# A separate buffer for the outgoing mLSTM states, and new durations for the gate chain in the mixer's list scheduler

## The chip, the cores and the metric

The kernel runs on one core of one Trainium2 chip. The time is that of one execution on the device in microseconds (us). The profile speaks of five engines: PE is TensorE (PEld its weight loads), DVE is VectorE, ACT is ScalarE, POOL is GpSimd and SP is SyncE, which here issues the DMAs. Each engine works through its own instructions in the order in which they were written, so an instruction that waits holds up all behind it on its engine.

## What is computed

One step of a two-layer hybrid diffusion backbone: a feed-forward half, a mixer, a second feed-forward half, for 512 latent tokens and 128 context tokens (640 columns in all), with 1024 features. The mixer projects its input once (`z = u @ w_in`) and splits the columns among grouped-query attention (A), a bidirectional matrix memory (B, mLSTM, 4 heads of 64) and differential attention (C). The part that the change touches is B. In the reference:

```
gates = (gb + b_gates).reshape(B, L, 4, H_B)
ig = gates[:, :, 0::2]
logf = log_sigmoid(gates[:, :, 1::2])
b = cumsum(logf);  m_out = max(b + m, max(dlog))      # per chunk, both directions
num = (q k^T * exp(dlog - m_out)) v + w_inter * (q C)
h = num / max(|den|, exp(-m_out))
C_new = decay * C + sum_s wk * k v                    # the final states
h_b = h_f + rev(h_r)
return h_b, (stack([Cf, Cr]), stack([nf, nr]), stack([mf, mr]))
```

For the context tokens the final states `C`, `n` and `m` of both directions are outputs (`new_b_C`, `new_b_n`, `new_b_m`).

## The kernel before

Activations are held feature by token. Every fp32 product is made of three passes of a high and a low half (`mm3`), which makes TensorE the engine with the most to do. Each layer runs feed-forward, mixer, feed-forward; the mixer appears twice in the trace, once per layer.

Inside the mixer the order of the work of PE, ACT, DVE and POOL is set by a list scheduler (`Sched`), at build time. Each piece of work is an `op(engines, ns, fn, deps, dl, alloc, use)`: engines that can do it, an assumed duration in ns, what it depends on, a due time, and the buffers that it allocates or uses. `Sched.run` repeatedly takes the op that could start earliest by these assumed durations (ties by due time) and writes out its instructions. So a duration in an `op` changes no instruction; it changes where instructions stand in each engine's queue, and on which of two allowed engines a copy is put.

Two places matter here.

*The gate chain* (`gates`). The gate columns are projected on PE (`gps`), biased on ACT into `ig` and `lf`, and then go back and forth in seven steps over rows of 640 tokens: `c1`, `c2` on ACT (log-sigmoid into `tm`), `c3` on DVE (four scans, `ae`), `c4` on DVE (four scans, the running maximum), `c5` on ACT (`nM`), `c6` on DVE (`tm` and the small `mo`, `Ml`), `c7` on ACT (a table load, `ae`, `ws`). Then PE transposes `ae` and `ws` into PSUM (`aet`, lines 1557 to 1566). Meanwhile PE multiplies the other columns of `w_in`: one token tile and column chunk (`zps`) is 24 matmuls of 512 columns, evacuated by a copy into `z`, which then goes through the rotary multiplications (`m`, `yc`, `kc`) and splits (`qsC`, `ks`) on POOL, DVE and ACT. The tiles `zps` have four PSUM buffers with the transposes (`ps1`).

*The final states and the second direction.* For the context tokens `kw` (DVE) scales the keys, four small matmuls per direction make the states in PSUM, ACT copies them into the SBUF tile `cst`, and two DMAs write it out, `new_b_C` in rows of 64 numbers and `new_b_n` in single numbers of 4 bytes (`stc`, lines 2133 and 2134). The tile `cst` and the tile `hx` share one buffer (tag `hx`, one copy of it). `hx` is the quotient of the second direction of each head, made on DVE (line 2101) and added to the first direction's `hb` by POOL (line 2104); then `hsq` on ACT, `hss` on DVE, `hrr` on POOL normalise the head. The assumed duration of `stc` is 2000 ns, on the pseudo-engine Q that stands for DMAs.

```
            xb = buf("hx")
            ...
            o = op("D", dve(320), hx, (o,), dl - 3, (xb,), (b,))
            self.out = op("G", gps(320), ..., (o, self.out), dl, use=(xb,))
        ...
        cb, cbx = buf("hx"), {}
        ...
        bops = [op("Q", 2000, stc, co, dl, use=(cb,))]
```

The functions `act(n)`, `dve(n)` and `gps(n)` give assumed durations for n columns: 60 + 0.84 n, 66 + 1.05 n and 150 + 2.1 n ns.

Of the kernel before, what the change touches and what calls it, by code (L numbers as in the profile page):

```python
# [10 lines left out]
F32 = mybir.dt.float32  # L11
# [6 lines left out]
D = 1024  # L18
# [4 lines left out]
T = LAT + CTX  # L23
# [38 lines left out]
class Sched:  # L62
# [32 lines left out]
    def buf(self, pool):  # L95
        return Buf(pool)

    def op(self, eng, ns, fn, deps=(), dl=0.0, alloc=(), use=()):

        o = Op()  # L100
        o.ns = {eng: ns} if len(eng) == 1 else dict(zip(eng, ns))
        o.fn, o.dl, o.alloc, o.id, o.end, o.succ = fn, dl, alloc, self.n, None, []
        self.n += 1
        self.left += 1
        o.deps = [d for d in deps if d is not None]
        o.wait = 0
        for d in o.deps:
            if d.end is None:
                d.succ.append(o)
                o.wait += 1  # L110
        for b in (*alloc, *use):
            b.users.append(o)
        if not o.wait:
            self.ready.append(o)
        return o
# [66 lines left out]
class Net:  # L182
# [958 lines left out]
    def mixer(self, l, np_stack):  # L1141
# [71 lines left out]
        for nm, g in (("tq", gq), ("tk", gk)):  # L1213
            tb = zp.tile([P, 4, 2, 64], F32, name=nm, bufs=1)
            nc.vector.tensor_tensor(tb[:, :, 0, :], self.ropeA[:, :, 0, :], g.unsqueeze(1).to_broadcast([P, 4, 64]), ALU.mult)
            for e in range(2):
                o = 1 - e
# [21 lines left out]
        S = Sched({k: RS[k] for k in "ps1 ps2 pr pT ks z sqz m2 qsC QTc KTC hsqC".split()})  # L1239
        op, buf = S.op, S.buf  # L1240
        act = lambda n: 60 + 0.84 * n
        dve = lambda n: 66 + 1.05 * n
# [239 lines left out]
        def gates(rawb, wb, prev, dl):  # L1482
# [11 lines left out]
            o = op("G", 2500, g0, prev, dl, (rawb,))  # L1494
            o, o2 = split_ops(lambda: bx["raw"], [P, KD, P], wb, rawb, bx, (o,), dl)
            outs = []
            for hf in range(2):
                c0, c1 = HALF[hf]
# [13 lines left out]
                o = op("P", 24 * 0.42 * (c1 - c0), pe, (o, o2), dl, (pb,), (wb,))  # L1512
# [29 lines left out]
                nc.scalar.activation(ae[64 : 64 + R], tm, AF.Exp)  # L1542
                nc.scalar.activation(ws, ae[0:R, LAT:T], AF.Exp, bias=Ml)

            o = op("A", 2 * act(T), c1, outs, dl)
            o = op("A", act(T) + 1300, c2, (o,), dl)
            o = op("D", 4 * dve(T) + 250, c3, (o,), dl)
            o = op("D", 2 * dve(T) + 250, c4, (o,), dl)
            o = op("A", act(T), c5, (o,), dl)
            o = op("D", dve(T) + 400, c6, (o,), dl)  # L1550
            o = op("A", act(T) + act(CTX) + 1500, c7, (o,), dl)
            pb = buf("ps1")

# [23 lines left out]
        def split_ops(get, shape, wb, rawb, bx, deps, dl):  # L1577
            def hi():
                if wb.slot < 4:
                    H, L = self.wpair(shape, wb.slot)  # L1580
                else:
                    H, L = (zp.tile(shape, F32R, tag="w5" + x, name="w" + x, bufs=1) for x in "HL")
                nc.scalar.copy(H, get())
                bx["hl"] = (H, L)

            def lo():
                H, L = bx["hl"]
                nc.vector.tensor_tensor(L, get(), H.bitcast(F32), ALU.subtract)

            o1 = op("A", act(1024), hi, deps, dl, (wb,), (rawb,))  # L1590
            o2 = op("D", dve(1024), lo, (o1,), dl, use=(wb, rawb))
            return o1, o2
# [21 lines left out]
        for ci, (parts, post) in enumerate(chunks):  # L1614
            if ci == 1:
                def cache():
                    nc.sync.dma_start(ka[0], a["cache_a_k"][0, l])
                    nc.sync.dma_start(va[0], a["cache_a_v"][0, l])
                    nc.sync.dma_start(kc[0], a["cache_c_k"][0, l].rearrange("s h n d -> s (h n) d"))
                    nc.sync.dma_start(vc[0], a["cache_c_v"][0, l])  # L1620

                o = op("Q", 3000, cache, (), 0.0)
                for k in ("ka", "va", "kc", "vc"):
                    done[k, 0] = o
                rb, wb = buf("raw"), buf("w")
                pops += gates(rb, wb, (), clock)
# [23 lines left out]
            for t in range(NT):  # L1650
# [6 lines left out]
                o = lastpe  # L1657
                for kk in range(4):
                    def pe(kk=kk, t=t, bx=bx, pb=pb, hls=hls):
                        if kk == 0:  # L1660
                            bx["ps"] = self.ps1("zps", pb.slot)
                        project_k(bx["ps"], t, hls[kk]["hl"], kk)

                    o = op("P", 6 * 214, pe, (o, *(hops[kk] or ())), clock, (pb,) if kk == 0 else (), (wbs[kk],) if kk == 0 else (wbs[kk], pb))
# [8 lines left out]
        tc_ = []  # L1673
# [182 lines left out]
        tp = tp_stack.enter_context(self.pool("mlstm", 2, side="right"))  # L1856
# [65 lines left out]
        for i, (dst, q) in enumerate(((hb, 0), (kb, 1), (vb[:, :, :, 0:64], 2), (ob, 3))):  # L1922
            for t0_, t1_ in ((0, 2), (2, 5)) if q != 2 else [(t, t + 1) for t in range(NT)]:
# [4 lines left out]
                o = op("Q", RL + 3000 * i + t0 * 1e3, ld, (), t0 - 50)  # L1928
# [177 lines left out]
        self_sel, self_mask, self_ps1, self_mm = self.sel, self.mask, self.ps1, self.mm  # L2106
        heads = [Head(h) for h in range(4)]

        cb, cbx = buf("hx"), {}
        co = []  # L2110
        for d in range(2):
            b, kwb = buf("ps1"), buf("hsqB")

            def kwf(d=d):
                if d == 0:
                    cbx["cst"] = tp.tile([64, 8, 65], F32, tag="hx", name="cst", bufs=1)
                cbx["kw", d] = kw = tp.tile([P, NT, 64], F32, tag="hsq", name="kw", bufs=1)
                for h in range(4):
                    nc.vector.tensor_scalar(kw[:, h, :], kb[:, 4, h, :], wsT[:, 32 * d + h : 32 * d + h + 1], None, ALU.mult)

            def pe(d=d, b=b):
                cbx["ps", d] = ps = self.ps1("cst", b.slot)
                for h in range(4):
                    self.mm(ps[0:64, h * 65 : h * 65 + 65], cbx["kw", d][:, h, :], vb[:, 4, h, :], True, True)

            dl = t0 + 45 + 3 * d
            o = op("D", 600, kwf, (lds[1, 4], *done["aeT"], *co), dl, (cb, kwb) if d == 0 else (kwb,), () if d == 0 else (cb,))
            o = op("P", 900, pe, (o, lds[2, 4]), dl, (b,), (kwb,))
            co.append(op("A", 300, lambda d=d: nc.scalar.copy(cbx["cst"][:, 4 * d : 4 * d + 4, :], cbx["ps", d][0:64, 0:260].rearrange("p (h c) -> p h c", c=65)), (o,), dl, use=(b, cb)))
# [69 lines left out]
        for dd in range(2):  # L2199
# [7 lines left out]
            for e in range(2):  # L2207
# [20 lines left out]
                o = None  # L2228
                for i, c in enumerate(CORD):
                    for hf in range(2):  # L2230
# [8 lines left out]
                        o = op("P", 3 * 0.418 * w, pe, (o, o2, *yts[c, hf], *scs), t0 + L2 + 30 + 10 * d + i, (pb,) if o is None else (), (wb,) if o is None else (wb, pb))  # L2239
# [165 lines left out]
```

## Time and profile before

| | us |
|---|---|
| median of three runs | 2797.31 (2794.95 to 2800.3) |
| the profiled execution | 2793.09 |
| its span, first to last instruction | 2791.3 |
| PE busy | 2700.6 (97% of the span) |
| DVE busy | 2128.1 (76%) |
| ACT busy | 1285.6 (46%) |
| POOL busy | 308.6 (11%) |

The profiled execution is one run of the same program; its trace has start and duration of each instruction, and for idle time in front of an instruction the event that ended it. Besides busy time a stretch has a granted clock of TensorE, 1.00 for 2.4 GHz and 0.50 for 1.2 GHz. A busy share is an average over the whole span. Idle time of an engine is read from the waits and from the stretch in which it lies.

### The profile page before, as it was taken

Reading aid. Unit: us, or ns where it says so; the run is one execution under the profiler, and the core shown is the slowest. Engines: PE = TensorE matmul, PEld = TensorE weight load, DVE = VectorE, ACT = ScalarE, POOL = GpSimd, SP = SyncE. Lnnn points to the kernel's source line nnn. Section 1 sums busy time; section 2 is a strip of 40 time slices with the busy share of each in tenths; the row PEclk is TensorE's granted clock in tenths of the full one; section 3 lists DMA queues with packets and bytes.
Section 4 is the critical chain, followed back from the end, with each engine's and each line's share of the span. In section 5 each row is a group of like instructions: output and inputs, shape, how many; then the busy total and the mean of one; then the engine's idle time right before and its main releaser. Section 6 shows DMA issues by size and latency. Waiting matters only on the chain.

```text
span 2791.3 us, 46818 instructions
## 1 busy us (share of the span) xinstructions
PE 2700.6 (97%) x17869; PEld 2533.9 (91%) x17869; DVE 2128.1 (76%) x4618; ACT 1285.6 (46%) x2941; POOL 308.6 (11%) x504
## 2 busy tenths in 40 slices
PE   7999999999989999999989999999999999999998
PEld 5998999888889999999989999997888898999998
DVE  6687899776865578898987889988667647676765
ACT  5424334456666342433444334345657644343433
POOL 1000000142522100000010000003343220000000
PEclk8999999999999999999999999999999999999999
DMA  8444443322102334344333443442211033222232
GB/s 239 138 145 141 119 129 107 110 93 88 40 3 80 96 95 137 91 121 122 105 91 92 121 144 109 141 131 83 82 50 39 3 114 91 77 75 76 84 84 76
DMA packets 363352, 276.44 MB, mean 99 GB/s; under 512 B 25128, under 2 KB 350840, under 8 KB 363128
## 3 DMA queue, kind: packets, MB, share of 16 engines
q1 hardware_dynamic: 363128, 273.45, 32.8%
q8 instruction: 141, 2.31, 0.4%
q14 instruction: 83, 0.68, 0.1%
HBM read 259.25 MB, written 14.16 MB: 98 GB/s over the span
## 4 chain that ended last, share of the span: by engine, by line
PE 86%; DVE 6%; ACT 3%; DMA 2%; POOL 2%; issue 1%; SPq 0%; POOLq 0%; DVEq 0%; ACTq 0%
PE gu L192 35%; PE w L192 20%; PE zps L192 6%; PE ga L192 5%; PE wo L192 4%; PE tr L1293 3%; PE y L192 3%; PE sc L192 2%; PE num L192 2%; PE z L192 1%; PE adp L333 1%; DMA out_new_b_n<-cst 1%; PE adt L348 1%; DMA adaw<-in_w_ada 1%; PE st L192 1%
## 5 line engine op out<-in xcount | busy, mean ns | idle before, releaser
L192 PE MATMUL gu<-u,wH 128*128 128x320 f32 x3504 | 624.8, 316 | 8.3 <-DVE pm L669 3.7
L192 PE MATMUL w<-hid,wH 128*128 128x384 f32 (+1 forms) x2816 | 624.4, 312 | 1.9 <-ACT wH L212 1.1
L192 PEld LDWEIGHTS gu<-u,wH 128*128 128x128 f32 x3504 | 541.9, 190 | 33.9 <-ACT X L1005 7.9
L192 PE MATMUL gu<-u,wL 128*128 128x320 f32 x3120 | 565.6, 314 | 2.4 <-DVE wL L213 1.1
L192 PEld LDWEIGHTS gu<-u,wL 128*128 128x128 f32 x3120 | 482.8, 189 | 20.6 <-ACT X L1005 6.7
L192 PEld LDWEIGHTS w<-hid,wH 128*128 128x128 f32 x2816 | 471.8, 188 | 7.3 <-ACT hid L693 3.4
L192 PE MATMUL w<-hid,wL 128*128 128x256 f32 (+1 forms) x1408 | 432.1, 311 | 0.9 <-DVE wL L213 0.8
L192 PEld LDWEIGHTS w<-hid,wL 128*128 128x128 f32 x1408 | 264.7, 189 | 2.5 <-DVE wL L213 2.3
L221 ACT CAST wH<-raw 128x512 fp32r<-128x512 f32 x266 | 163.6, 620 | 205.5 <-PE w L192 91.8
L345 DVE SCALAR_TENSOR_TENSOR adacc<-adaw,cs,adacc 128x256 f32<-128x256 f32 x602 | 255.0, 477 | 0.0
L192 PE MATMUL zps<-wH,u 128*128 128x512 f32 x704 | 244.6, 408 | 1.9 <-ACT u L887 1.8
L738 POOL TENSOR_TENSOR ssum<-ssum,sq 128x384 f32<-128x384 f32 (+1 forms) x36 | 36.2, 1005 | 1899.6 <-ACT sq L737 1807.3
L221 ACT CAST wL<-raw 128x512 fp32r<-128x512 f32 x266 | 163.9, 620 | 167.1 <-PE gu L192 55.7
L930 DVE SCALAR_TENSOR_TENSOR h<-w,mod,h 128x128 f32<-128x128 f32 (+1 forms) x384 | 154.8, 434 | 108.2 <-PE w L192 106.8
L212 ACT CAST wH<-raw 128x640 fp32r<-128x640 f32 (+2 forms) x148 | 120.4, 816 | 226.1 <-PE w L192 165.6
L222 DVE TENSOR_TENSOR wH<-raw,wH 128x512 fp32r<-128x512 f32 x266 | 182.0, 686 | 41.5 <-ACT wH L221 39.8
L222 DVE TENSOR_TENSOR wL<-raw,wL 128x512 fp32r<-128x512 f32 x266 | 182.0, 686 | 38.4 <-ACT wL L221 37.3
L192 PEld LDWEIGHTS zps<-wH,u 128*128 128x128 f32 x704 | 133.8, 191 | 34.0 <-ACT u L887 5.3
L213 DVE TENSOR_TENSOR wL<-raw,wH 128x640 fp32r<-128x640 f32 (+2 forms) x148 | 137.4, 931 | 28.8 <-PE gu L192 14.7
L693 ACT CAST hid<-th 128x320 fp32r<-128x320 f32 x176 | 80.8, 459 | 148.4 <-DVE th L688 148.0
L192 PE MATMUL zps<-wL,u 128*128 128x512 f32 x352 | 139.6, 397 | 0.0
L1701 DVE TENSOR_REDUCE mx<-sc 128x1 f32<-128x640 f32 (+1 forms) x160 | 110.5, 707 | 27.0 <-PE sc L192 26.8
(338 smaller groups left out, 4428.8 us busy)
## 6 DMA issues: line engine op xcount, KB each, us to landing
raw<-in_w_ff_in SPq DMA_DIRECT2D x176, 512.0 KB
adaw<-in_w_ada SPq DMA_DIRECT2D x144, 512.0 KB
raw<-in_w_ff_out SPq DMA_DIRECT2D x32, 768.0 KB
raw<-in_w_ff_out SPq DMA_DIRECT2D x32, 640.0 KB
rawi<-in_w_in SPq DMA_DIRECT2D x16, 1024.0 KB
rawo<-in_w_out SPq DMA_DIRECT2D x8, 1024.0 KB
bspill<-z SPq DMA_DIRECT2D x20, 256.0 KB
rawi<-in_w_in SPq DMA_DIRECT2D x8, 512.0 KB
```

The source lines that it names most:

```text
L192: self.nc.tensor.matmul(out, lhsT, rhs, start=start, stop=stop, skip_group_check=go_on)
L212: nc.scalar.copy(H, raw)
L213: nc.vector.tensor_tensor(L, raw, H.bitcast(F32), ALU.subtract)
L221: nc.scalar.copy(w[:, 0], raw)
L222: nc.vector.tensor_tensor(w[:, 1], raw, w[:, 0].bitcast(F32), ALU.subtract)
L333: self.nc.tensor.matmul(ps[j : j + 32, 0:256], self.cs32[:, k, :], raw, start=k < 4, stop=k >= 4, tile_position=(0, j))
L345: nc.vector.scalar_tensor_tensor(acc[v], raw, col, acc[v], ALU.mult, ALU.add)
L693: nc.scalar.copy(self.hid[q][:, 0, c], st["th", hf])
L738: (nc.gpsimd if d in SSG else nc.vector).tensor_tensor(ssum[:, :w], ssum[:, :w], sq[:, :w], ALU.add)
L930: nc.vector.scalar_tensor_tensor(hh, ps[:, s0:s1], gm[:, v, d : d + 1], hh, ALU.mult, ALU.add)
L1293: nc.tensor.transpose(pt[:, i * P : (i + 1) * P], x, ident)
L1701: nc.vector.tensor_reduce(bx["mx"], view(), AX.XY, ALU.max, negate=True)
```

## The change

The tile `cst` gets a tag and a buffer of its own (`cst`, in the attention pool), so `hx` no longer shares with it. In the scheduler the assumed durations of `c1`, `c2`, `c3`, `c4` and `c6` change: for 640 tokens `c3` goes from 3202 to 5476 ns, `c4` from 1726 to 3300 ns, `c6` from 1138 to 1888 ns, `c1` and `c2` grow by 300 and 150 ns. No operation is added or removed.

```diff
-            o = op("A", 2 * act(T), c1, outs, dl)
-            o = op("A", act(T) + 1300, c2, (o,), dl)
-            o = op("D", 4 * dve(T) + 250, c3, (o,), dl)
-            o = op("D", 2 * dve(T) + 250, c4, (o,), dl)
+            o = op("A", 2 * act(T) + 300, c1, outs, dl)
+            o = op("A", act(T) + 1450, c2, (o,), dl)
+            o = op("D", 2 * dve(T) + 4000, c3, (o,), dl)
+            o = op("D", 3300, c4, (o,), dl)
             o = op("A", act(T), c5, (o,), dl)
-            o = op("D", dve(T) + 400, c6, (o,), dl)
+            o = op("D", dve(T) + 1150, c6, (o,), dl)
...
-        cb, cbx = buf("hx"), {}
+        S.grow("cst", 1)
+        cb, cbx = buf("cst"), {}
...
-                    cbx["cst"] = tp.tile([64, 8, 65], F32, tag="hx", name="cst", bufs=1)
+                    cbx["cst"] = tc_[0].tile([64, 8, 65], F32, tag="cst", name="cst", bufs=1)
```

The queues change at the same two places in both layers. The first place is PE at the transposes of the gate chain, in the first layer's mixer (`aet` are those transposes, `zps` the projections, `tr<-ident,ks` the transposes of a split key tile). Before:

```order
L192 MATMUL zps<-wL,u 128x512
L192 MATMUL zps<-wH,u 128x512
L1557 MATMUL aet<-ident,ae 128x100 x4
L1565 MATMUL aet_6328<-ident,ae 128x100
L1566 MATMUL aet_6328<-ident,ws 128x36
L1293 MATMUL tr<-ident,ks 128x128 x2
L192 MATMUL zps<-wH,u 128x512
```

and in the changed kernel, again around `aet`:

```order
L192 MATMUL zps<-wL,u 128x512
L192 MATMUL zps<-wH,u 128x512
L1557 MATMUL aet<-ident,ae 128x100 x4
L1565 MATMUL aet_6375<-ident,ae 128x100
L1566 MATMUL aet_6375<-ident,ws 128x36
L1293 MATMUL tr<-ident,qsC 128x128 x2
L192 MATMUL zps<-wH,u 128x512
```

The two transposes of `ks` and one whole projection of 24 `zps` matmuls, which stood behind `aet`, now stand ahead of it; what follows `aet` is the transposes of `qsC` and the next projection.

On ACT at the same place, between `c2` (line 1520) and the first exponential of `c7` (line 1542):

```order
 L1520 ACTIVATE tm<-tm 36x640
+L1251 COPY z<-zps 128x512 x2
+L1531 ACTIVATE nM<-ig 36x640
+L1251 CAST qsC<-yc 128x64 x3
 L1251 COPY z<-zps 128x512
-L1531 ACTIVATE nM<-ig 36x640
-L1251 CAST qsC<-yc 128x64 x4
+L1251 CAST KTC<-tr 128x2x128
+L1251 CAST qsC<-yc 128x64
+L1251 CAST ks<-kc 128x2x32 x2
 L1542 ACT_TABLE_LOAD
 L1542 ACTIVATE ae<-tm 36x640
```

A second evacuation `z` comes ahead of `nM` (DVE did it, behind the scans), and a third evacuation, the copy `KTC` and the two `ks` casts come ahead of the table load and `ae`. On DVE that evacuation `z<-zps`, just ahead of `tm` (line 1534), gives its place to one rotary multiplication `yc<-z,tcq`.

The second place is `hx`. On DVE, in the first head's second direction:

```order
 L2087 TENSOR_TENSOR den<-den,aeT 128x5
 L2088 RECIPROCAL den<-den 128x5
-L1261 TENSOR_SCALAR qa_5897<-y,rcA 128x64
+L2101 TENSOR_TENSOR hx<-num,den 128x320
 L1255 COPY pT<-tr 128x256
 L1255 CAST QT<-tr 128x512
```

`hx` now stands right behind the reciprocal that it needs; it stood some fifteen instructions later, behind the `Dd` multiplications. Its follower `hb<-hb,hx` moves up on POOL, and `hrr` on POOL moves ahead of two pairs of `hlb` splits. On ACT around the second copy into `cst`, before:

```order
L1251 CAST qs<-qa_5894 128x4x64
L1707 ACTIVATE pr,sums<-sc,mx 128x640
L2129 COPY cst<-cst 64x260
L1251 COPY pT<-tr 128x384
L1251 CAST QKb<-tr 128x3x128
```

and in the changed kernel (its lines are one higher here):

```order
L1251 CAST qs<-qa_5894 128x4x64
L1707 ACTIVATE pr,sums<-sc,mx 128x640
L1759 ACTIVATE hsq<-hb 128x320
L2130 COPY cst<-cst 64x260
L1251 CAST QKb<-tr 128x3x128
L1251 CAST hlb<-hb 128x64
```

The square `hsq`, which waits for POOL's `hb`, now stands ahead of the copy of `cst` and of the evacuations behind it; the copy `pT` of 384 columns has gone to DVE.

## Rows read from the trace of the kernel before

**Rows 1.** The page: busy us, share of the span, instructions of each engine.
```profile
PE 2700.6 (97%) x17869; PEld 2533.9 (91%) x17869; DVE 2128.1 (76%) x4618; ACT 1285.6 (46%) x2941; POOL 308.6 (11%) x504
```

**Rows 2.** Waits of PE, whole span: us in total, times, longest.
```profile
PE st L192 <- DVE hx L2101: 14.2, 2, 7.3
...
PE aet L1557 <- POOL qsC L1273: 7.0, 2, 3.7
PE yt L2175 <- DVE u L2185: 4.8, 2, 2.4
...
PE sc L192 <- ACT pr L1707: 2.6, 2, 1.3
```

**Rows 3.** The chain that ended last, the first layer's piece: start, us, what.
```profile
799.49 9.23 DMA out_new_b_n<-cst
```

**Rows 4.** Timeline at `hx`: start, us, engine, instruction, idle before, releaser.
```profile
795.17 0.19 DVE L2088 RECIPROCAL den<-den 128x5 f32<-128x5 f32 x1
...
808.84 0.49 DVE L2101 TENSOR_TENSOR hx<-num,den 128x320 f32<-128x320 f32 x1 [7.64 <-DMA out_new_b_n<-cst]
...
809.39 1.22 PE L192 MATMUL st<-QKb 128*128 128x512 f32 x2 [7.29 <-DVE hx L2101]
...
2177.15 1.22 PE L192 MATMUL st<-QKb 128*128 128x512 f32 x2 [6.92 <-DVE hx L2101]
```

**Rows 5.** Stretches behind the four stalls: us, busy by engine, granted clock.
```profile
587.22:592.00 4.78, 4.78 (x18) 3.80 (x19) 4.73 (x10) 1.79 (x7) 4.36 (x9) 0.64 0.00 0
809.40:813.90 4.50, 4.50 (x18) 3.90 (x19) 2.55 (x11) 2.40 (x9) 3.21 (x6) 0.53 0.00 0
1954.00:1960.40 6.40, 6.40 (x20) 5.02 (x21) 4.67 (x10) 1.76 (x7) 4.42 (x9) 0.50 0.01 1
2177.10:2182.30 5.20, 5.15 (x21) 4.55 (x22) 3.15 (x11) 2.54 (x10) 3.50 (x6) 0.50 0.00 0
```

**Rows 6.** Timeline of the gate chain's end, first layer, as in rows 4.
```profile
583.76 0.42 DVE L1348 TENSOR_TENSOR yc<-yc,m 128x256 f32<-128x256 f32 x1
583.76 0.74 ACT L1531 ACTIVATE nM<-ig 36x640 fp32r<-36x640 f32 x1 [8.40 <-DVE ig L1480]
...
584.44 0.68 DVE L1255 COPY z<-zps 128x512 f32<-128x512 f32 x1
...
585.09 1.28 ACT L1542 ACT_TABLE_LOAD   x1
...
586.39 0.73 ACT L1542 ACTIVATE ae<-tm 36x640 f32<-36x640 f32 x1
...
586.83 0.45 DVE L1348 TENSOR_TENSOR kc<-kc,m 128x256 f32<-128x256 f32 x1
...
587.22 0.53 PE L1557 MATMUL aet<-ident,ae 100*128 100x100 f32 x4 [3.26 <-POOL qsC L1273]
...
588.26 0.68 DVE L1348 TENSOR_TENSOR yc<-yc,m 128x256 f32<-128x256 f32 x1
...
588.69 0.39 ACT L1251 CAST ks<-kc 128x64 fp32r<-128x64 f32 x2
```

**Rows 7.** Stretch of steady projections ahead of it, columns as in rows 5.
```profile
567.00:584.00 17.00, 16.96 (x78) 13.81 (x76) 13.49 (x20) 7.85 (x14) 5.41 (x7) 1.00 0.40 137
```

**Rows 8.** Timeline of the gate chain's end, second layer.
```profile
1950.50 0.74 ACT L1531 ACTIVATE nM<-ig 36x640 fp32r<-36x640 f32 x1 [8.39 <-DVE ig L1480]
...
1953.96 0.90 PE L1557 MATMUL aet<-ident,ae 100*128 100x100 f32 x4 [3.73 <-POOL qsC L1273]
```

**Rows 9.** Stretches ahead of the `hx` stall and behind it, as in rows 5.
```profile
797.00:802.10 5.10, 5.10 (x43) 4.29 (x42) 3.07 (x11) 4.44 (x17) 1.26 (x3) 1.00 0.21 26
...
830.00:840.00 10.00, 10.00 (x80) 9.56 (x80) 8.08 (x22) 7.28 (x23) 4.50 (x8) 1.00 0.00 1
```

**Rows 10.** Timeline: the square `hsq` of the first head.
```profile
810.32 0.47 ACT L1759 ACTIVATE hsq<-hb 128x320 f32<-128x320 f32 x1 [7.77 <-POOL hb L2104]
```

**Rows 11.** The stretch behind the wait for `yt`, as in rows 5.
```profile
890.00:892.00 2.00, 2.00 (x10) 2.00 (x9) 1.43 (x5) 1.88 (x6) 2.00 (x2) 0.50 0.00 1
```

## The prediction

> **What bounds the kernel now.** I read the page first: PE is busy for 97% of the span [rows 1]. So a change of order pays only where PE stands still, or runs slow, and the second view is the list of PE's waits. The reader is to see there that the longest sum is `st` behind `hx`, 14.2 us in two waits, and that `aet` has 7.0 us in two [rows 2]; the program has two mixers, so each is one wait per layer. These are the two places that the change touches. The chain of waits then says what is behind the first: the write of `new_b_n` lies on the chain for 9.23 us [rows 3], and once more in the second layer. The timeline shows the mechanism. The reciprocal that `hx` needs starts at 795.17 and takes 0.19 us; `hx` starts only at 808.84, when the DMA out of `cst` has released their common buffer; PE's next `st` starts at 809.39 after 7.29 us of nothing, and the second layer repeats it with 6.92 us [rows 4].
>
> For `aet` the list names a POOL instruction as releaser, but the timeline shows the true one: `ae` on ACT runs from 586.39 for 0.73 us, thus to 587.12, and `aet` starts at 587.22 [rows 6]. PE had reached it 3.26 us earlier, at 583.96, while ACT's `nM` started only at 583.76 because of DVE's scans, and the subtraction, the table load and the exponential were still to come. The second layer waits 3.73 us [rows 8].
>
> The last view is the granted clock. Behind each stall PE is busy, but not at 2.4 GHz: 0.64 over 4.78 us, 0.53 over 4.50, 0.50 over 6.40 and 0.50 over 5.20 [rows 5]. At clock c a stretch of length t does the work of c·t, so these lose 1.7 + 2.1 + 3.2 + 2.6 = 9.6 us more. The price of the four stalls is therefore 3.26 + 7.29 + 3.73 + 6.92 = 21.2 us of standing still and 9.6 us of half clock, 30.8 us together.
>
> **The change part by part.** Nothing is added or removed, so no instruction costs more by itself.
>
> *The buffer of its own.* `hx` now needs only the reciprocal, done at 795.4 [rows 4], and stands right behind it. The DMA still takes its 9 us, but who waits for it next is the next tenant of `cst`'s memory, at the mixer's end: the DMA lands at 808.7 [rows 3], and the stretch of `yt` begins about 80 us later [rows 11]. That stretch is its cover; without it the cost would be today's 7 us. So the 7.29 and 6.92 us end, unless another instruction is late there. What could be: ACT was busy for 4.44 of the 5.10 us ahead of the stall [rows 9], so in the closed-up order it has little room, and the square `hsq`, 0.47 us [rows 10], now stands ahead of the `cst` copy, the `QKb` casts and a `pT` copy for which PE's transposes, `st` and `y` wait, while POOL does `hrr` before two pairs of splits. Such a wait is not in the trace of before at this place. From below its cost is nothing: from 830 to 840 us PE was busy for all 10 us with ACT at 7.28 and DVE at 8.08 [rows 9], which is the same mixture of work. From above I take the longest wait of PE on ACT's queue, 1.3 us [rows 2]. I take 1.0 per layer, near the upper end, since `hsq` and `hrr` both moved ahead of work for PE: 2.0 in all.
>
> *The gate chain's durations.* PE now does two transposes and one projection before `aet`. Pace: the stretch ahead holds 72 projections and 6 shorter ones in 16.96 us [rows 7]; counting the short ones half, one takes 0.226, and 24 take 5.4 us. With about 0.3 for the transposes PE reaches `aet` at 583.96 + 5.7 = 589.7. When is `ae` ready? `nM` is not earlier, since the scans are not. On DVE the evacuation of 0.68 us ahead of `tm` gives way to a multiplication of 0.42 to 0.68 (the two lengths in which such an instruction appears, [rows 6]), so `kc`, which ended at 587.28, ends between 587.0 and 587.3. ACT's two `ks` casts wait for it and take 0.39, then come the table load, 1.28, and `ae`, 0.73 [rows 6]: 587.0 + 0.1 + 2.4 = 589.5 at the early end, 589.8 at the late one. So PE and `ae` arrive together; I take no wait in the first layer. In the second, `nM` starts 0.27 after PE's arrival (1950.50 against 1953.96 − 3.73 = 1950.23, [rows 8]) where it was 0.20 ahead in the first, so `ae` is 0.5 later relative to PE: I take 0.3. The bounds are 0 and 1.3, as above. Behind `aet` on PE stand the `qsC` transposes and the next projection; `aeT` itself is read only tens of us later. The evacuation that DVE gives up costs ACT one copy, which falls into ACT's idle 8.40 us ahead of `nM` [rows 6]; without that cover it would delay `nM` by its length. The new order thus pays no instruction on the gate path but the casts, and those run under the projection.
>
> *What the clock gives back.* After a stall of 3 us or more every stretch fell to the low level [rows 5]; if no such stall is left, the 9.6 us return too. Smaller waits are not harmless: `yt`'s, 2.4 us [rows 2], was followed by 0.50 as well [rows 11]. Waits of 1.0 and 0.3 are the smallest of these, and I take the clock as staying high.
>
> The page "TensorE: Matmul & The Clock Gate" of the Trainium skill, section "A second HAM failure mode: psum-queue depth-cycling", says that frequent short idling between groups of matmuls makes the clock swing between its two levels. By that rule the left-over waits could cost the clock even though each is short, and only the standing time would come back; rows 11 agree in that a wait well under the four stalls was enough. It is the first rival below.
>
> The page "SBUF — State Buffer" of the Trainium skill, section "Who interferes with whom", says that a VectorE instruction with two inputs in SBUF and a GpSimd instruction that reads SBUF exclude each other for their whole length. The trace agrees at least in kind: the same multiplication takes 0.42 or 0.68 us [rows 6]. By this rule POOL's work at the gates could hold up both `tm` and `kc`; at the 0.26 us that the rows show for one such meeting, `ae` would come 0.5 later in each layer, and the sum would be 27.5 instead of 28.5.
>
> *Sum.* 30.8 − 2.0 − 0.3 = 28.5 us. Against the profiled execution, 2793.1 (1.8 more than its span), that gives 2764.6. The median of the runs shown is 4.2 us above that execution, so I put the median of the changed kernel at 2797.3 − 28.5 = 2768.8, and forecast **2768 us**. All that follows a mixer starts from its end: the reload of `h` and the weights of the next half are issued when the mixer's buffers come free, so they move along.
>
> **The rivals.**
>
> *A. The clock does not come back, or the small waits are larger.* Each place keeps a wait of about 1.3 us and the clock still falls behind it, with the smallest of the four losses, 1.7: 4 × 3.0 = 12 us left, 2797.3 − 18.8 = 2778. If only the standing time returned, it would be 2797.3 − 21.2 = 2776. For it: rows 11. Against it: in the stretch from 830 to 840 us [rows 9], and in five more of ten us from 820 to 880, the same mixture of work left PE busy throughout at 1.00.
>
> *B. One place works and the other doesn't.* If `ae` is again late at `aet` by as much as before, because the casts ahead of the table load wait for DVE and POOL, only the `hx` part counts: 7.29 + 6.92 + 2.1 + 2.6 − 2.0 = 16.9, 2780. If `hx` found another late releaser, only the gates count: 3.26 + 3.73 + 1.7 + 3.2 − 0.3 = 11.6, 2786. Against both: the releasers in the rows are named and each is cut.
>
> *C. Nothing changes:* `hx` stays behind a DMA because the new tile's memory or the output write holds it in another way, and `aet` stays late by the casts: 2797. For it speaks only that an order shows no times.
>
> *D. Slower.* ACT becomes late between the heads: `hsq` waits for POOL's `hb`, and behind it in ACT's queue stand the evacuations that free the four PSUM buffers. If POOL's `hb` came late, PE would run out of buffers at this place and stand. The gates and the cut waits give 30.8 us, so it turns the sign from 15.4 us of standing per layer on, against 7.29 now; the place holds 4.44 us of ACT work [rows 9], so it would need a delay of POOL that no row shows. With 20 us per layer it would be 2797.3 − 30.8 + 40 = 2806.
>
> **How the numbers follow.** Forecast 0.74, its own range 2763 to 2774 (no wait left gives 2766.5 on the median and 2762.3 on the profiled execution; 1.3 at each place, clock kept, gives 2771.7 on the median). A 0.13, B 0.07, C 0.03, D 0.03. The range reaches to A and the first case of B and leaves about one in ten out: **2760 to 2782**. About 0.2%, 5.6 us, is what a measurement of this kernel can tell from no change: faster 0.94, same 0.03, slower 0.03.
>
> **What would show it.** In the changed trace: no wait of PE on `hx`, and `hx` starting within 1 us of its reciprocal; the DMA of `new_b_n` off the chain; `aet` behind 24 more projections with a wait under 0.6 us in both layers; the granted clock at 1.00 behind both places; PE's idle between the first head and the second at most 1.3 us per layer. The prediction is wrong if a new wait for `QKb`, `pT` or `hlb` near 798 to 806 us exceeds 2 us, if the clock falls there all the same, or if the feed-forward halves take longer by what the mixers gain.

## The result and the profile after

The changed kernel takes 2764.48 us, the median of four runs (2761.12 to 2766.94), against 2796.13 (2792.28 to 2800.3) for the kernel before beside it: a ratio of 0.9890, 95% interval 0.9879 to 0.9902, thus 27.4 to 33.8 us less. The profiled execution took 2766.94, the slowest of the four, with a span of 2765.2 us, 26.1 less than the span before.

The page first: PE busy, share and instructions, as in [rows 1]. PE's busy time, which the half clock lengthens, fell by 5.6 us; the other 20.5 us by which the span is shorter were idle time of PE.

```profile
PE 2695.0 (97%) x17869; PEld 2529.0 (91%) x17869; DVE 2129.0 (77%) x4616; ACT 1285.1 (46%) x2943; POOL 310.4 (11%) x504
```

The list of PE's waits shows what went and what did not; its columns are those of [rows 2].

```profile
PE yt L2176 <- DVE u L2186: 4.8, 2, 2.4
...
PE sc L192 <- ACT pr L1707: 2.6, 2, 1.3
...
PE tr L1293 <- POOL ks L1273: 2.0, 5, 0.7
```

`st` behind `hx`, first in [rows 2], and `aet`, 7.0 us there, are no longer in it, while the waits of `yt` and `sc` are what they were. The last line has grown: `tr` behind `ks` was 1.2 us before. The timeline at the first place, to be laid beside [rows 4]:

```profile
792.17 0.19 DVE L2088 RECIPROCAL den<-den 128x5 f32<-128x5 f32 x1
792.46 0.49 DVE L2101 TENSOR_TENSOR hx<-num,den 128x320 f32<-128x320 f32 x1
793.03 0.86 POOL L2104 TENSOR_TENSOR hb<-hb,hx 128x320 f32<-128x320 f32 x1 [14.49 <-DVE hx L2101]
...
795.63 0.47 ACT L1759 ACTIVATE hsq<-hb 128x320 f32<-128x320 f32 x1
796.00 0.35 ACT L2130 COPY cst<-cst 64x260 f32<-64x260 f32 x1
...
797.09 0.63 SPq L2135 DMA_DIRECT2D out_new_b_n<-cst  x1
...
802.23 0.52 PE L1293 MATMUL tr<-ident,hlb 128*128 128x128 f32 x3 [0.27 <-ACT qa L1259]
```

`hx` starts 0.1 us after its reciprocal and 4.6 us before the write of `new_b_n` is even issued. Between the first head and the second PE waits once, 0.27 us. At the gate chain, beside [rows 6]:

```profile
583.64 0.74 ACT L1531 ACTIVATE nM<-ig 36x640 fp32r<-36x640 f32 x1 [4.74 <-DVE ig L1480]
...
584.94 1.07 DVE L1534 TENSOR_TENSOR tm<-nM,lf 36x640 f32<-36x640 f32 x1
...
585.60 0.39 ACT L1251 CAST ks<-kc 128x64 fp32r<-128x64 f32 x2
586.02 1.28 ACT L1542 ACT_TABLE_LOAD   x1
586.59 0.46 DVE L1348 TENSOR_TENSOR kc<-kc,m 128x256 f32<-128x256 f32 x1
587.31 0.74 ACT L1542 ACTIVATE ae<-tm 36x640 f32<-36x640 f32 x1
...
589.28 0.51 PE L1557 MATMUL aet<-ident,ae 100*128 100x100 f32 x4
```

`aet` has no wait: `ae` ended at 588.05, 1.2 us ahead of PE (0.7 in the second layer). The stretches behind the two places, to be read against [rows 5]; the number behind POOL's busy time and count is the granted clock:

```profile
590.00:596.00 6.00, 6.00 (x29) 4.90 (x29) 5.30 (x10) 4.25 (x9) 4.37 (x9) 1.00 0.00 0
797.00:806.00 9.00, 8.73 (x70) 8.00 (x68) 7.91 (x27) 8.15 (x33) 5.42 (x11) 1.00 0.14 17
1941.00:1947.00 6.00, 5.85 (x30) 4.55 (x29) 4.94 (x9) 3.59 (x9) 5.80 (x12) 1.00 0.02 4
2146.00:2158.00 12.00, 11.66 (x93) 10.30 (x92) 10.49 (x34) 9.95 (x37) 6.38 (x12) 1.00 0.10 13
726.00:740.00 14.00, 12.08 (x57) 10.21 (x58) 10.72 (x28) 10.20 (x35) 9.68 (x15) 0.63 0.64 169
2080.00:2092.00 12.00, 11.47 (x54) 9.89 (x54) 9.05 (x25) 8.71 (x32) 8.21 (x15) 0.57 0.63 169
```

All four are at 1.00, where they were at 0.50 to 0.64. The last two rows are another place, the start of the last attention scores, where PE waits 1.3 us for `pr`, as it did before. There the two profiles differ:

```profile
730.50:744.50 14.00, 11.49 (x71) 9.01 (x70) 11.84 (x30) 10.34 (x36) 10.42 (x16) 0.88 0.68 174
2098.00:2110.00 12.00, 10.25 (x53) 8.41 (x54) 10.89 (x29) 9.80 (x35) 9.13 (x15) 0.72 0.80 219
```

Those are the same stretches of the kernel before. At clock c a stretch t loses (1 − c)·t: 1.7 and 3.4 us before, 5.2 and 5.2 after. So in these two executions 5.3 us of what the gates gave is missing again further on. The views of single tiles give the same by stage. Their lines have the durations of one instruction (shortest, median and longest, in ns), then the first and the last start (us). First the kernel before, then the changed one, first layer:

```profile
L192 PE MATMUL gps<-u,wH x32: 279/308/336, 560.5 to 567.2; 128*128 128x384 f32 x16, 128*128 128x256 f32 x16
L192 PE MATMUL st<-QKb x40: 273/397/792, 770.1 to 867.9; 128*128 128x512 f32 x32, 128*128 128x128 f32 x8
L2175 PE MATMUL yt<-ident,qa x20: 272/347/475, 889.3 to 895.6; 128*128 128x128 f32 x20
```

```profile
L192 PE MATMUL gps<-u,wH x32: 279/308/336, 560.2 to 567.0; 128*128 128x384 f32 x16, 128*128 128x256 f32 x16
L192 PE MATMUL st<-QKb x40: 274/397/502, 767.1 to 856.1; 128*128 128x512 f32 x32, 128*128 128x128 f32 x8
L2176 PE MATMUL yt<-ident,qa x20: 270/273/328, 877.5 to 882.7; 128*128 128x128 f32 x20
```

From the last `gps` to the first `st` the first layer took 202.9 us before (567.2 to 770.1) and 200.1 after, the second 204.7 and 200.6: 6.9 less, and 12.2 with the 5.3 put back. From the first `st` to the first `yt` of a `qa` it took 119.2 and 119.3 before, 110.4 and 110.4 after: 17.7 less. The remaining 1.5 us lie elsewhere. Whether the 5.3 belong to the change is a question for the experiments (the ninth).

### The profile page after: what moved, and what is told of

It reads as the page before. It is cut to its first block, busy times and chain, and to the rows that moved or that the text cites. A ratio compares the mean times of both kernels' runs of the same rounds, so it can differ in the third digit from the quotient of the medians.

```text
span 2765.2 us, 46833 instructions
## 1 busy us (share of the span) xinstructions
PE 2695.0 (97%) x17869; PEld 2529.0 (91%) x17869; DVE 2129.0 (77%) x4616; ACT 1285.1 (46%) x2943; POOL 310.4 (11%) x504
## 4 chain that ended last, share of the span: by engine, by line
PE 86%; DVE 6%; ACT 3%; POOL 2%; issue 1%; DMA 1%; SPq 0%; POOLq 0%; DVEq 0%; ACTq 0%
PE gu L192 35%; PE w L192 21%; PE zps L192 7%; PE ga L192 5%; PE wo L192 4%; PE tr L1293 3%; PE y L192 3%; PE sc L192 2%; PE num L192 2%; PE z L192 1%; PE adp L333 1%; DVE adacc L345 1%; PE adt L348 1%; DMA adaw<-in_w_ada 1%; PE st L192 0%
```

## The experiments

The theory: the two places are independent stalls of order, and each returns its standing time and the half clock behind it. The rivals: the clock does not return, one place depends on the other, the buffer itself (and not the order) is what matters, or a longer assumed duration costs something later. Each time is a median beside the kernel before on the same chip (2793.98 to 2796.9).

**1 and 2. One part alone.** The first kernel has only the buffer, the second only the durations; of each the main line.

```diff
-        cb, cbx = buf("hx"), {}
+        cb, cbx = buf("cst"), {}
```

```diff
-            o = op("D", 4 * dve(T) + 250, c3, (o,), dl)
+            o = op("D", 2 * dve(T) + 4000, c3, (o,), dl)
```

> The kernel before with the buffer of its own for cst alone; the gate chain keeps its old durations. Theory (the two places are independent, and each gives back its standing time and the half clock behind it): 14.2 us of standing and 4.7 of half clock less about 0.6 of left-over waits, so 18 us less, 2778; no wait of PE on hx, aet still waits 3.3 and 3.7 us. Rival 1 (the clock does not come back at this place): 13.6 less, 2782.5. Rival 2 (the place is only free together with the new gate order): 2790 or more.

> The kernel before with the new gate durations alone; cst and hx share the buffer as before. Theory: 7.0 us of standing and 4.9 of half clock come back, 11.6 less, 2784.5; no wait of PE on aet, st still waits 7 us twice behind hx. Rival (part of it is given back further on: the trace of the changed kernel shows 2.7 and 4.1 us from the gates to the first st of each layer, and a longer half-clock stretch at the start of the last attention scores): 6.8 less, 2789.

Measured: the buffer alone 2776.94 us, ratio 0.9931 (0.9918 to 0.9943), 20.0 less; the durations alone 2786.32, ratio 0.9968 (0.9956 to 0.9980), 10.6 less. Together 30.6, and the whole change gave 31.7 on medians: they add. The waits of PE, of the buffer alone and then of the durations alone:

```profile
PE aet L1557 <- POOL qsC L1273: 6.8, 2, 3.4
```

```profile
PE st L192 <- DVE hx L2101: 14.7, 2, 7.5
```

Each kernel keeps the other's stall. The buffer took away 14.2 us of standing and gave 20.0, with an interval of 15.9 to 22.9: both the standing time alone and the first rival's 13.6 lie outside it, so the clock comes back there. The durations took away 7.0 and gave 10.6; their interval, 5.6 to 12.3, contains 7.0 and the rival's 6.8, so the time does not decide. The stretches behind the gates in the second kernel's own trace do: they stand at 1.00.

```profile
590.00:592.00 2.00, 2.00 (x10) 1.63 (x11) 1.29 (x3) 1.18 (x6) 2.00 (x5) 1.00 0.00 0
...
1954.00:1956.00 2.00, 2.00 (x12) 1.55 (x11) 1.29 (x3) 1.43 (x6) 2.00 (x5) 1.00 0.00 0
```

The longer wait of `tr` behind `ks` comes with the durations: 2.1 us in the second kernel, 0.6 in the first.

**3 and 4. What makes the buffer matter.** Third, the shared buffer stays and only the told duration of the write changes; fourth, only `n` leaves the shared tile (ACT's copy out of PSUM becomes two).

```diff
-        bops = [op("Q", 2000, stc, co, dl, use=(cb,))]
+        bops = [op("Q", 11000, stc, co, dl, use=(cb,))]
```

```diff
+                    cbx["cn"] = tc_[0].tile([64, 8, 1], F32, tag="cn", name="cn", bufs=1)
...
-            nc.sync.dma_start(a["new_b_n"][0, l].rearrange("d h (k o) -> k (d h) o", o=1), cst[:, :, 64:65], allow_slow_non_contiguous=True)
+            nc.sync.dma_start(a["new_b_n"][0, l].rearrange("d h (k o) -> k (d h) o", o=1), cbx["cn"], allow_slow_non_contiguous=True)
```

> The kernel before, with the shared buffer, but the scheduler is told that the write of the states takes 11000 ns instead of 2000. Theory: the stall is one of order, not of memory: hx is put behind other work of DVE, PE finds other work too, and the 14.2 us go without a buffer: 16 less, 2780, no wait of PE on hx over 1 us. Rival: hx must still come some 10 us late, the first head holds its PSUM buffers so long, and PE waits for a buffer or for the next head's tiles instead: 2785 to 2795 with waits of 3 us or more at the same place.

> The kernel before, order and gates as they were; only the column n leaves cst for a small tile of its own (the copy out of PSUM becomes two copies), so hx shares its buffer with the write of C in rows of 64 numbers and no longer with the write in single numbers of 4 bytes. Theory: the 4-byte write is what holds the buffer: hx starts within 2 us of PE's arrival, PE's waits on hx fall from 7.3 to under 2 us each, 2779 to 2783. Rival: any write out of the shared buffer holds it about as long, waits on hx stay over 5 us and the time at 2794 to 2798.

Measured: 2777.02 us (0.9919 to 0.9944) and 2775.93 (0.9914 to 0.9940), the same as the buffer alone; both came out some 3 us better than expected. In the third kernel the timeline shows `hx` 17 us after its reciprocal, behind other work, with no idle time of DVE ahead of it:

```profile
795.18 0.19 DVE L2088 RECIPROCAL den<-den 128x5 f32<-128x5 f32 x1
...
812.63 0.48 DVE L2101 TENSOR_TENSOR hx<-num,den 128x320 f32<-128x320 f32 x1
```

So a late `hx` costs nothing by itself (from the first `st` to the last `wo`, the products of the mixer's output, the two layers take 173.4 and 172.4 us, with the buffer alone 173.5 and 171.8); a DVE queue that stands still for it does. The third kernel answers for the first place: it was a stall of order, and memory one cure of two. In the fourth the chain of waits (start, us, what) and the timeline show whom `hx` waits for now:

```profile
801.04 2.77 DMA out_new_b_C<-cst
803.86 0.04 issue
803.90 0.50 DVE hx L2101
```

```profile
803.90 0.49 DVE L2101 TENSOR_TENSOR hx<-num,den 128x320 f32<-128x320 f32 x1 [0.44 <-DMA out_new_b_C<-cst]
```

The write of `C`, 128 KB a layer, took 2.77 us on the chain; that of `n`, 2 KB in as many pieces of 4 bytes each as `C` has rows, 9.23 [rows 3]. PE's wait on `hx` is gone from the list, and the rival (any write holds the buffer as long) is out.

**5 and 6. How exact the durations must be.** Fifth, of the new durations only that of `c3` (`c1` and `c2`, not shown, go back as well); sixth, `c6` told 5 us too long.

```diff
-            o = op("D", 3300, c4, (o,), dl)
+            o = op("D", 2 * dve(T) + 250, c4, (o,), dl)
...
-            o = op("D", dve(T) + 1150, c6, (o,), dl)
+            o = op("D", dve(T) + 400, c6, (o,), dl)
```

```diff
-            o = op("D", dve(T) + 1150, c6, (o,), dl)
+            o = op("D", dve(T) + 6150, c6, (o,), dl)
```

> The changed kernel with the new duration of c3 alone; c1, c2, c4 and c6 go back to their old ones. Its queues put aet behind 84 projection matmuls since gps (72 before, 96 in the changed kernel), and the table load and ae stand ahead of the copy KTC and of the two ks casts. Theory (the wait at aet is ae's end less PE's arrival, and any order that brings the two within some tenths is as good): ae ends 0.8 us earlier than in the changed kernel, about 587.2, PE arrives 12 projections or 2.7 us earlier, about 586.6, so aet waits 0.7 us in the first layer and about as much in the second, and the clock stays up behind it: 2764 to 2767. Rival (even such a wait makes the clock fall): 1.4 of standing and 3 to 5 of half clock more, 2769 to 2771.

> The changed kernel with c6 told 5 us too long: aet stands behind 120 projection matmuls since gps instead of 96, and a 1024-column cast of weights stands ahead of ae on ACT. Theory: ae is ready several us before PE comes, there is nothing left to gain, and aeT is read only tens of us later, so nothing to lose: 2762 to 2767, no wait on aet. Rival (what was put ahead of aet is missing as cover later, or the gate vectors come late for the first decays): 2768 to 2775, with a new wait of PE of 2 us or more between 600 and 770 us.

Measured: 2772.75 us (0.9907 to 0.9935) and 2763.54 (0.9879 to 0.9906). The fifth is slower than both expectations, the rival's 2769 to 2771 being the nearer one. Its timeline has the wait of `aet` as expected, and a second that my expectation lacked, for the evacuation `z` that frees the PSUM buffer of the last transposes; behind both the clock fell:

```profile
587.97 0.56 PE L1557 MATMUL aet<-ident,ae 100*128 100x100 f32 x4 [0.49 <-ACT ae L1542]
...
589.66 0.30 PE L1565 MATMUL aet<-ident,ae 100*128 100x100 f32 x1 [1.13 <-DVE z L1255]
```

```profile
590.00:596.00 6.00, 6.00 (x21) 4.72 (x22) 3.53 (x9) 0.87 (x3) 3.31 (x7) 0.72 0.00 0
```

1.6 us of waits in two pieces cost another 1.7 of clock, 3.3 us per layer (1946 to 1952 shows 0.72 too); by 3.3 in both layers, 6.6 of the 8 us by which it is slower than the changed kernel are told. In the sixth `ae` ends at 594.98 and `aet` starts at 595.78 without a wait: told too long, `c6` costs nothing here; told too short, `c1`, `c2`, `c4` and `c6` together do.

**7. The cover.** The write of `new_b_n` is issued twice.

```diff
+            nc.sync.dma_start(a["new_b_n"][0, l].rearrange("d h (k o) -> k (d h) o", o=1), cst[:, :, 64:65], allow_slow_non_contiguous=True)
```

> The changed kernel with the write of new_b_n issued twice (the same values to the same place), so cst's buffer is held for some 18 us instead of 9. Theory: the write lies under about 80 us of work of the mixer, nothing waits for it: 2762 to 2767, no new wait of PE. Rival (it is hidden only just, by the queue of SP or by the next owner of cst's memory): 2768 or more, with a wait on a DMA behind it.

Measured: 2765.14 us (0.9884 to 0.9911), no new wait of PE. SP issues the first write at 795.4 us and the second only at 804.5, when the first has landed:

```profile
L2136 SPq DMA_DIRECT2D out_new_b_n<-cst x2: 595/595/595, 804.5 to 2159.0; - x2
```

So the theory holds for a buffer held twice as long; how much of the 80 us could be used, the run does not show.

**8. The next place.** `wH` waits for the last `kc` also in the scheduler's view, so the casts `u` go ahead of it.

```diff
...
-                o1 = op("A", act(1024), hi, (prev,), wd, (wb,), (rb,))
+                o1 = op("A", act(1024), hi, (prev, done["b", 3]), wd, (wb,), (rb,))
...
-                o2 = op("G", gps(1024), lo, (o1,), wd, use=(wb, rb))
+                o2 = op("DG", (dve(1024), gps(1024)), lo, (o1,), wd, use=(wb, rb))
```

> The changed kernel with the same treatment given to the next place of this kind, the wait of yt behind the casts u (2.4 us per layer): on ACT the cast wH of the output weights stood ahead of the u casts and waited 1.1 us for DVE's kc, which the scheduler did not know. The cast wH now depends on the last head's kc, and the split wL may go to DVE too. The u casts then stand ahead of it. Theory: they start at 874.4 instead of 876.4, the next yt about 1.6 us earlier, 3.2 us less in two layers, and 1 to 2 of half clock in the layer where it follows: 2759 to 2762. Rival (wH comes 0.5 us later and wo then waits for wL instead): no gain, 2763 to 2766, with a wait of wo of 1 us or more per layer.

Measured: 2767.67 us (0.9895 to 0.9922), no gain, and 1.7 us above the rival's range. PE's waits in the first layer between 871 and 887 us:

```profile
PE yt L2176 <- DVE u L2186: 1.3, 2, 0.8
PE wo L192 <- DVE wL L2220: 0.3, 1, 0.3
```

The wait of 2.4 us shrank to 0.8 and came back in pieces, for `u` and for `wL`. From the first `yt` to the last `wo` the layer took 65.0 us (875.0 to 940.0) against 64.8 in the changed kernel's profile; but that is the shortest value, and the second layer there and both layers of the ninth run below took 66.3, against 65.1 in the second layer here. So the stretch itself did not lose, and in three of four comparisons won 1.2 or 1.3 us. The rival was right that nothing is gained, but not in its cause: the wait on `wo` is 0.3 us, not 1. Where the time went is open.

**9 to 12. The changed kernel again, the cure without a buffer, and more durations told truly.**

> The changed kernel once more, unaltered, beside the three others on one chip: 2762 to 2767. The half clock behind the wait of sc for pr (728 us and 2080 us) cost between 1.7 and 5.1 us a layer in the profiles so far, with the same wait of 1.3 us ahead of it; theory: this varies from execution to execution and is no part of the change. Rival: in the changed kernel it is always 5.1.

> The new gate durations, no buffer of its own for cst, but the write of the states told as 11000 ns instead of 2000. Theory: what the buffer gave was an order in which nothing waits behind the write, and the true duration gives one too: 2763 to 2768, as fast as the changed kernel. Rival (with the gates changed as well the later hx is missed): 2770 or more with a wait of PE of 2 us or more between 795 and 830 us.

> The changed kernel with the durations of the attention steps told as the trace shows them too: the exponential pr 220 ns longer, its maximum mx 75 ns, the small cf step 200 ns, the differential sum pr 135 ns. Theory (it is again an order made for durations that were too short): the wait of sc for pr (1.3 us a layer), those of tr for pr (1.1 us a layer) and the half clock behind the first (1.7 to 5.1 us a layer) shrink, 4 to 10 us less, 2755 to 2761. Rival (at that place PE lacks other work, DVE is busy throughout, and no order helps): 2762 to 2768, waits of the same size at other names.

> As the one before, and POOL's steps too (the power rr from 1120 ns to 1640 for 8 columns and 690 for 2, the rotary products m by half longer). Theory: the last projections' way through POOL is put earlier, ks and KTA come in time: 2753 to 2760, the waits of tr for ks (2 us in all) gone as well. Rival: 2762 to 2768 or slower, since each of these orders only trades one wait for another.

The tenth joins the edit of the third kernel to the durations. The edits of the eleventh, and what the twelfth adds:

```diff
-            o = op("D", dve(n), mx, (o,), dl, use=(b,))
+            o = op("D", dve(n) + 75, mx, (o,), dl, use=(b,))
-            return bx, op("A", act(n) + 180, ex, (o,), dl, prs if first else (), (b,) if first else (b, prs[1]))
+            return bx, op("A", act(n) + 400, ex, (o,), dl, prs if first else (), (b,) if first else (b, prs[1]))
...
-            c = op("D", 400, c1, (e0, e1), dl)
-            o = op("D", 1.04 * n + 130, c2, (c,), dl, use=(p0, p1))
+            c = op("D", 600, c1, (e0, e1), dl)
+            o = op("D", 1.04 * n + 265, c2, (c,), dl, use=(p0, p1))
```

```diff
-            o = op("G", 1120, pw, (o,), dl)
+            o = op("G", 380 + 157 * n, pw, (o,), dl)
...
-            o1 = op("G", 2 * gps(n * hw), swap, deps, dl, (mb,), (zb,))
+            o1 = op("G", 2 * (1.5 * gps(n * hw)), swap, deps, dl, (mb,), (zb,))
```

Measured: the changed kernel again 2765.72 us (0.9877 to 0.9908); without the buffer 2770.0 (0.9892 to 0.9919); the attention durations 2776.49 (0.9917 to 0.9942); POOL's as well 2768.34 (0.9887 to 0.9914).

The ninth lies in its range of 2762 to 2767 and settles the 5.3 us. At the start of the last scores its profile shows

```profile
724.00:738.00 14.00, 12.12 (x70) 9.99 (x68) 12.52 (x32) 11.25 (x39) 9.41 (x15) 0.76 0.67 190
2078.50:2090.50 12.00, 9.54 (x56) 7.05 (x55) 10.55 (x27) 9.61 (x35) 9.77 (x15) 0.86 0.69 196
```

so 3.4 and 1.7 us there, where the same program lost 5.2 and 5.2 in the first profile. Its stages from `gps` to `st` are 198.3 and 198.4 us, 10.9 less than before; from `st` to `yt` 110.9 and 110.5, 17.1 less; its span is 27.9 shorter. How long the clock stays low behind one and the same wait varies between executions, and so did the kernel with the durations alone (5.2 and 1.7).

The tenth is 4 us slower than the changed kernel on the same chip, at the edge of the rival's 2770, but with none of the rival's waits. The longest wait of PE from the first `st` to the first `yt`:

```profile
PE tr L1293 <- ACT pr L1707: 0.4, 1, 0.4
```

From `st` to `yt` it takes 112.0 and 111.3 us, 1.9 more than the ninth; but it wins this back at once, for from the first `st` to the last `wo` it takes 173.1 and 172.4 against 173.7 and 173.2. So in these profiles the 4 us do not lie at the place of the buffer. The two spans differ by 5.4 us: 3.6 more lie in the stages from `gps` to `st`, where its half clock at the start of the last scores cost 5 us in each layer against 3.4 and 1.7 in the ninth, and 3.2 more lie outside the two mixers. Whether the clock falls so in every execution of it is open, and so is whether the buffer is worth the 4 us.

The eleventh is slower than both its expectations (2755 to 2761, and 2762 to 2768): the wait of `sc` for `pr` shrank from 2.6 to 0.4 us, but `tr` behind `pr` grew from 2.3 us to

```profile
PE tr L1293 <- DVE pr L1832: 5.8, 7, 2.0
```

and from the first `st` to `yt` it takes 112.6 us in each layer, from `gps` to `st` 202.9 and 202.4, more than the changed kernel in both stages. The twelfth, with POOL's steps told too, went to its rival (2762 to 2768 or slower). It has 198.8 and 198.3 us from `gps` to `st` but 112.5 in each layer from `st` to `yt`: the first stage is as good as in the ninth run, the second is not. Truth for some steps made a worse order than the understatement that it replaced. No version here beats the changed kernel by more than the measurement can tell.

## Why the prediction was right

*Standing time, 21.2 us.* Right: the four waits are gone from the list, idle time of PE fell by 20.5 us, and the parts add (20.0 and 10.6).

*Half clock, 9.6 us.* Right: the four stretches stand at 1.00, the buffer alone gave more than its standing time by more than its interval, and with the durations alone the trace has 1.00 behind both gates. Rival A, with the clock staying low, is out for the whole change: its 18.8 us lies below the interval of 27.4 to 33.8. The rows on which A rested were nevertheless telling: in the fifth run 1.6 us of waits in two pieces were enough. The page "TensorE: Matmul & The Clock Gate" of the Trainium skill, section "A second HAM failure mode: psum-queue depth-cycling", which stood beside A, agrees in kind with that run (0.72 behind waits of 0.49 and 1.13 us). The changed kernel is no case of it: it has one wait of 0.27 us there, and the clock stayed at 1.00.

*Left-over waits, 2.0 at `hx` and 0.3 at `aet`.* Too large: 0.27 us in the first layer, 0.34 us of idle PE from 2146 to 2158 in the second, none at `aet`. I had taken a value near the upper end because `hsq` and `hrr` moved ahead of work for PE; `hsq` found its operand ready, since POOL's `hb` had ended 1.7 us before (793.89 against 795.63).

*`ae` and PE arrive together.* Wrong by 1.2 us to the good side. PE came at 589.3 (I said 589.7), but `ae` was done at 588.05 instead of 589.5. The failed step is "ACT's two `ks` casts wait for it": they ran at 585.60, before that `kc` (586.59), since they belong to an earlier one, and the table load waited for nothing. Nor did POOL decide `ae` by holding up DVE: `tm` had ended at 586.01, and `ae` started when the table load was over, at 587.30. The fifth run shows what this margin was worth. One wait had no term: `tr` behind `ks` grew by 0.8 us with the new gate order.

*DMA covered by 80 us.* Right as far as it was tried: a second write behind the first cost nothing.

*B, C and D.* B needed one place to fail; both work alone. C is out, since both waits are gone. For D nothing came late: `hb` follows `hx` by 0.1 us.

*Sum.* 28.5 us forecast, 31.7 measured on medians with an interval that contains it; the profile of the ninth run has 10.9 and 17.1 us at the two places, where the terms said 11.6 and 16.9. That it fits so closely is in part luck: with the 0.6 us of waits that were found instead of 2.3, the terms would have said 30.2 and the two places gave 28.0, so a left-over that was taken too large stood in for a return that was smaller than its full price. The forecast time was 3.5 us too high, yet not by these terms. The span of the ninth run is 27.9 shorter; the medians differ by more, because the profiled execution of the kernel before was 3.0 us faster than its median, and why executions of that kernel differ so is not shown.

## What to carry to other kernels

In a list-scheduled kernel a wait that the scheduler does not know is paid by everything queued behind it: look for the instruction that starts the moment a DMA lands, and give the scheduler the measured duration, or take the shared buffer away. Here either did by itself; together with the new gate durations the buffer came out 4 us ahead, for a reason that is open. Price such a wait with the half clock behind it, read from the same trace, and where an order is to be set by durations, err on the long side for steps that others wait for, as the sixth run did without loss. But a truer table is not by itself a better order: correcting the attention steps alone cost 11 us, so each set has to be run.

## What the runs showed of the hardware

The write of 512 single numbers held its buffer three times as long as that of 512 rows of 64 (9.23 us against 2.77 on the chain). It was not moving data for most of this: in the trace of the kernel before, all the packets recorded for the two writes, 1056 in that stretch, lie between 800.0 and 801.4 us, none follows until `hx` starts, and the buffer came free only at 808.7. What passes in the 7.3 us between is not shown.

The page "DMA: Bandwidth & Descriptors" of the Trainium skill, section "Specifications", puts the least size of a transfer for line rate at 512 bytes; the pieces of both writes (4 and 256 bytes) are below that, and it does not tell them apart, so the rows decide.

Behind the same wait of 1.3 us, in the same program, the granted clock's loss was 5.2 us in one execution and 1.7 or 3.4 in another. Two profiles are therefore compared place by place, and only medians of several runs as a whole.
